# A row norm in a decoder trunk: rstd on all partitions from one product with ones, and a power over 128x256

## The chip, the cores and the metric

The kernel runs on one core of a Trainium2 chip. The metric is the device time of one execution in microseconds (us). A core has TensorE (PE in the profile, its weight loads PEld), VectorE (DVE), ScalarE (ACT), GpSimd (POOL) and SyncE (SP), which issues the transfers. Each engine takes its instructions in order; an instruction that waits holds everything behind it on its engine.

## The reference

A two-layer decoder trunk on one sequence of 256 tokens and 1024 features, in f32. Layer 0 mixes tokens with latent attention (MLA), layer 1 with a Mamba-2 scan (SSD); each mixer stands between two SwiGLU networks of half a step. So there are six sub-layers, numbered s = 0 to 5 here: FFN, MLA, FFN, FFN, SSD, FFN. Each begins with the norm

```
def rms_norm(x, gain):
    y = xf * lax.rsqrt(jnp.mean(xf * xf, axis=-1, keepdims=True) + EPS)
    return y * gain
def modulate(x, gain, mod):
    return rms_norm(x, gain) * (1 + mod[:, None, 1]) + mod[:, None, 0]
...
    x = x + 0.5 * m[:, None, 0, 2] * swiglu(h, ffn_w_gu[i, 0], ffn_w_down[i, 0])
```

and the SSD mixer ends with the same norm over each of 4 groups of 512 gated features, before its output projection. The number that the change is about is rstd = (mean of squares + EPS) to the power -1/2: one number for each token, and for the groups one for each token and group.

## The kernel before

Features lie on the 128 partitions and the 256 tokens run along a tile, so x is 8 tiles of 128x256 and a sum over features is a sum over partitions. Weights come as 1 MB transfers, two pieces of 128x1024 each. A piece is split into a rounded part `whi` (ACT, L205) and the rest `wlo` (DVE, L206), and each product is done in three (`mm3`), so one piece, a 128-wide output tile, is 24 products on PE. `piece()` keeps two pieces split ahead of the one in use.

A sub-layer doesn't wait for its norm. While the sub-layer before leaves x (`leave_chunk`), `enter_chunk` makes raw tiles x times scale, and the squares of x are summed over the 8 tiles into `ssum` (128x256). The first products run on these raw tiles with two extra columns for the shift; their results are multiplied by the rstd row `R` (128x256, the same on every partition) on the way out of PSUM (L421, L523, L526, L764, L1125). Meanwhile `norm_chunks` makes normalised tiles `X2` out of x and R (L421, ACT L422, split L328 and L329), and from the sixth pair of FFN tiles on (NDEF), or the sixth SSD tile (SDEF), the products run on those.

R is made in these steps, at the head of s = 1 to 5:
- `rstd_cols`: two PE products with `ssum` as weights and one column of ones (128x1 each) put the sums of the tokens on partitions; DVE L435 makes mean plus EPS on 128x2; POOL L439 takes the power on 128x2.
- `spread`: two products of that column, broadcast to 128 wide, with the identity bring it back as a row on all partitions (128x256 in PSUM).
- `spread_row`: ACT L453 copies it to SBUF as R.

The four gates of SSD (`gate(g)`, generators that are stepped between the projections and then between the pieces of the output projection `down`) do the same for their groups: squares on ACT (L1419), sums on POOL or DVE (L1423), `rstd_cols`, some steps later `spread`, then L1434 multiplies four tiles by the row in PSUM, and four splits make the input of the output projection. MLA has two further `rstd_cols` (L435, L439 again) for its latents; they stay.

The order of each engine's instructions is made by a scheduler when the program is built: an instruction is taken when its inputs are expected to be ready, except where `order` or `pin` keeps the written order. DVE's queue holds the weight splits L206, the modulation sums L236, the readers of R and the splits of the tiles, all in one line.

Of the kernel before, what the change touches and what calls it, by code (L numbers as in the profile page):

```python
# [12 lines left out]
ALU = mybir.AluOpType  # L13
AX = mybir.AxisListType

D = 1024
T = 256
# [4 lines left out]
EPS = 1e-6  # L22
# [41 lines left out]
class Trunk:  # L64
# [349 lines left out]

    def norm_chunks(self, s, R, ms):

# [25 lines left out]
    def spread(self, r):  # L442
# [4 lines left out]
                             start=True, stop=True)  # L447
        return ps

    def spread_row(self, r):  # L450
        ps = self.spread(r)
        R = self.small([128, T], "R", 1)
        self.nc.scalar.copy(out=R, in_=ps[:, 0:T])  # L453
        return R

# [74 lines left out]
    def ffn(self, s):  # L530
        H = []

        def evac(banks, R):
            H.append(self.split_act(self.ffn_act(banks[0], banks[1], R)))

        if s == 0:
            X, prev = self.open_first(lambda banks: evac(banks, None))
            prevR = None
            j0 = NOPEN
        else:  # L540
            X = self.Xn
            prev = self.proj_first(X, [128, 128])
            r = self.rstd_cols([self.ssum], D)
            X2 = []
            j0 = 1
        for j in range(j0, NJ):
            if s == 0 and j == SETUP_AT:
                self.mla_setup()
            if s and j == NDEF:
                X = X2  # L550
            cur = []
            for i in range(2):
                w = self.piece()
                ps = self.bank()
                self.proj(ps, w, X)
                cur.append(ps)
                if s and j == 1 and i == 0:
                    prevR = R = self.spread_row(r)
                if s and i and 1 <= j < NDEF:
                    X2 += self.norm_chunks(s, R, part(j, NDEF))  # L560
            evac(prev, prevR)
            if s and j == NDEF:
                prevR = None
            if not s or j > NDEF:
                self.ada_half(1 if s else 2)
            prev = cur
        self.down(s, NJ, lambda k: H[k], [lambda: evac(prev, None)], 2, 1, 2)
# [226 lines left out]
    def mla(self, s):  # L794
        nc = self.nc
# [9 lines left out]


        kvp = self.proj_first(X, [128, 128])
        r = self.rstd_cols([self.ssum], D)
        rp = self.bank()
        self.proj(rp, self.piece(), X, 32)  # L810
        R = self.spread_row(r)
        qp = [self.bank()]
        self.proj(qp[0], self.piece(), X)
        kv = [self.latent(kvp[i], R, i) for i in range(2)]
# [531 lines left out]
    def ssd(self, s):  # L1346
        nc = self.nc
        X, X2 = self.Xn, []
        scans, gates = [], []
        done = dict(conv=0, scan=-1, z=0, gate=0)  # L1350

        def step(n=1):

            self.pin = True
            for _ in range(n):
                for line in (scans, gates):
                    if line is gates and done["gate"] >= done["scan"]:
                        continue
                    while line:
                        try:  # L1360
                            next(line[0])
                            break
                        except StopIteration:
                            line.pop(0)
                            done["scan" if line is scans else "gate"] += 1
                            if line is gates:
                                break
            self.pin = False

        pend, raws, xs_all, Z, G = [], [], [], [], []  # L1370
        dst = []
        dtp, ps = self.proj_first(X, [32, 128])
        r = self.rstd_cols([self.ssum], D)
        R = None

        pair = {}

        def evac(kind, i, ps, deferred, direct=False):

            if i % 2 == 0:  # L1380
                pair[kind] = self.slot()
            c0 = (i % 2) * T
            v = pair[kind][:, c0:c0 + T]
            open_pair = [t for t in raws if t[0] is pair[kind]]
            if open_pair:
                open_pair[0][2] = c0 + T
            elif not direct:
                raws.append([pair[kind], c0, c0 + T])
            if kind == "c":
                g, q = divmod(i, 6)  # L1390
                self.conv_evac(ps, R if deferred else None, (16 + g, 20 + g, 4 * g, 4 * g + 1, 4 * g + 2, 4 * g + 3)[q], v)
                dst.append(v)
            else:
                nc.scalar.activation(out=v, in_=ps[:, 0:T], func=AF.Silu if direct else AF.Copy)  # L1394
                Z.append(v)

        def flush():

            for t, c0, c1 in raws:
                self.order(nc.scalar.activation(out=t[:, c0:c1], in_=t[:, c0:c1], func=AF.Silu))  # L1400
            raws.clear()
            done["z"] = len(Z)

        opened = []

        def open_gates():
            while len(opened) < done["conv"] and done["z"] >= 4 * (len(opened) + 1):
                gates.append(gate(len(opened)))
                opened.append(1)

        def gate(g):
            sqs = []
            for ch in range(4 * g, 4 * g + 4):
                y = xs_all[ch]
                nc.vector.tensor_tensor(out=y, in0=y, in1=Z[ch], op=ALU.mult)
            yield
            for i in range(4):
                sq = self.t1()
                nc.scalar.activation(out=sq, in_=xs_all[4 * g + i], func=AF.Square)  # L1419
                sqs.append(sq)  # L1420
            add = nc.vector if g > 1 else nc.gpsimd
            for i in range(3):
                add.tensor_tensor(out=sqs[0], in0=sqs[0], in1=sqs[i + 1], op=ALU.add)  # L1423
            yield
            yield
            r = self.rstd_cols(sqs[:1], 512)
            yield
            yield
            ps = self.spread(r)
            yield  # L1430
            for i in range(4):
                ch = 4 * g + i
                y = xs_all[ch]
                nc.vector.scalar_tensor_tensor(out=y, in0=y, scalar=self.sng[:, ch:ch + 1], in1=ps[:, 0:T],  # L1434
                                               op0=ALU.mult, op1=ALU.mult)
                if i == 1:
                    yield
            for i in range(4):
                G.append(self.split_act(xs_all[4 * g + i]))
                if i == 1:  # L1440
                    yield

        order, c, z = [], 0, 0
        for kind in SSD_ORDER:
            order.append((kind, c if kind == "c" else z))
            c, z = c + (kind == "c"), z + (kind == "z")
        for n, (kind, i) in enumerate(order):
            step(SSD_STEPS[0])
            if n:
                ps = self.bank()  # L1450
                self.proj(ps, self.piece(), X)
            if n == 1:
                R = self.spread_row(r)
            if n == DT_AT:
                scans.append(self.ssd_dt(dtp, R))
            if pend:
                evac(*pend.pop(0))
            pend.append((kind, i, ps, n < SDEF, c == 24 and kind == "z" and i >= ZRAW))
            if 1 <= n < SDEF:
                X2 += self.norm_chunks(s, R, part(n, SDEF))  # L1460
            if n == SDEF - 1:
                X = X2
            step(SSD_STEPS[1])
            if dst and len(dst) % 6 == 0 and len(dst) // 6 > done["conv"]:
                g = done["conv"]
                flush()
                cv = dst[6 * g:]
                xs_all += cv[2:]
                scans.append(self.ssd_group(g, cv[0], cv[1], cv[2:]))
                done["conv"] += 1  # L1470
                open_gates()
            if kind == "z" and i == ZRAW:
                flush()
            if kind == "z" and i >= ZRAW:
                done["z"] = len(Z)
                open_gates()
                self.ada_half()

        def last_evac():
            evac(*pend.pop(0))  # L1480
            done["z"] = len(Z)
            open_gates()

        def finish():
            while scans or gates:
                step()

        def until(n):
            while len(G) < n:
                step()  # L1490
        self.down(s, 16, lambda k: G[k], [last_evac] + [step] * SSD_HOOKS + [finish], 4, SSD_EARLY, 1, SSD_EVERY,
                  [(lambda: until(8), 8), (lambda: until(12), 12)])
# [95 lines left out]
```

## Time and profile before

| | us |
|---|---|
| three runs | 1088.69, 1090.51, 1090.56; median 1090.51 |
| profiled execution | 1090.35 |
| its span in the trace | 1088.6 |
| PE busy | 1067.0 (98%) |
| DVE busy | 871.5 (80%) |
| ACT busy | 627.4 (58%) |
| POOL busy | 40.2 (4%) |

The span is first to last instruction of the profiled execution; 1.75 us of its time lie around it. Busy shares are means over stages. A row of a grouped view gives busy us, the mean ns of one instruction and the idle time of the engine before them with what ended it. A row of a timeline gives start, length, engine, line, operation, tiles and count, and in brackets the idle time before.

### The profile page before, as it was taken

The numbers are of one execution on the slowest core, as the hardware profiler recorded it, in microseconds if no ns is written. First come the engines' busy times: TensorE is split into PE (matmuls) and PEld (weight loads), VectorE is DVE, ScalarE is ACT, GpSimd is POOL, SyncE is SP. The second block draws the span as 40 slices with busy tenths as digits, with TensorE's granted clock in tenths as the row PEclk, the third lists the DMA queues.
The fourth block names the chain that finished last, engine by engine and source line by source line (L and its number), as shares of the span: only waits on it lengthen the run. The fifth ranks groups of instructions, "written<-read, shape, count | busy, mean of one in ns | idle before, by whom it ended". The sixth has DMA issues, their size and how long they took to land.

```text
span 1088.6 us, 21773 instructions
## 1 busy us (share of the span) xinstructions
PE 1067.0 (98%) x8830; PEld 1047.5 (96%) x8830; DVE 871.5 (80%) x1551; ACT 627.4 (58%) x1106; POOL 40.2 (4%) x102
## 2 busy tenths in 40 slices
PE   6999999999999999999999999999999999999998
PEld 5999999998899999999999999999999899999998
DVE  5889998789889888766999886599997788756642
ACT  4564544467667454444754444498898766544431
POOL 0000010000000000000000000000211000000000
PEclk9999999999999999999999999999999999999999
DMA  9988998755266788775699886544344456556630
GB/s 352 345 318 335 349 343 325 257 202 194 81 229 233 285 329 286 284 287 194 232 345 356 332 328 251 172 177 156 117 136 155 141 179 217 200 214 216 233 131 20
DMA packets 38264, 259.59 MB, mean 238 GB/s; under 512 B 4370, under 2 KB 5522, under 8 KB 8084
## 3 DMA queue, kind: packets, MB, share of 16 engines
q1 hardware_dynamic: 38164, 258.21, 65.1%
q8 instruction: 69, 1.13, 0.4%
q14 instruction: 31, 0.25, 0.1%
HBM read 257.14 MB, written 1.05 MB: 237 GB/s over the span
## 4 chain that ended last, share of the span: by engine, by line
PE 90%; ACT 4%; DVE 4%; DMA 1%; issue 0%; SPq 0%; ACTq 0%
PE bank L294 89%; DVE raw L258 2%; PE bank L299 1%; DVE wlo L613 1%; DMA cst<-in_cst_dram 1%; ACT whi L625 1%; ACT whi L205 1%; ACT sl L663 0%; ACT L1394 0%; ACT L1249 0%; ACT dec L1268 0%; ACT t L993 0%; ACT L1268 0%; ACT dec L1249 0%; DVE dec L1272 0%
## 5 line engine op out<-in xcount | busy, mean ns | idle before, releaser
L294 PE MATMUL bank<-sl,whi 128*128 128x256 f32 (+2 forms) x5360 | 957.5, 282 | 2.8 <-ACT whi L205 1.5
L294 PEld LDWEIGHTS bank<-sl,whi 128*128 128x128 f32 (+1 forms) x5360 | 820.0, 188 | 5.9 <-ACT whi L205 1.9
L294 PE MATMUL bank<-sl,wlo 128*128 128x256 f32 (+2 forms) x2680 | 749.9, 282 | 1.6 <-DVE wlo L206 0.9
L205 ACT CAST whi<-raw 128x1024 fp32r<-128x1024 f32 (+1 forms) x329 | 341.2, 1040 | 314.0 <-PE bank L294 224.2
L294 PEld LDWEIGHTS bank<-sl,wlo 128*128 128x128 f32 (+1 forms) x2680 | 504.6, 189 | 3.7 <-DVE wlo L613 2.4
L206 DVE TENSOR_TENSOR wlo<-raw,whi 128x1024 fp32r<-128x1024 f32 (+1 forms) x329 | 397.5, 1212 | 96.7 <-ACT whi L205 95.1
L236 DVE SCALAR_TENSOR_TENSOR raw<-raw,cb 128x1024 f32<-128x1024 f32 x128 | 154.8, 1219 | 23.9 <-DMA raw<-in_adaw_dram 23.8
L328 ACT CAST sl<-t 128x256 fp32r<-128x256 f32 x125 | 48.7, 402 | 27.6 <-DVE t L520 18.8
L329 DVE TENSOR_TENSOR sl<-t,sl 128x256 fp32r<-128x256 f32 x125 | 50.9, 416 | 1.3 <-ACT sl L328 1.3
L459 DVE SCALAR_TENSOR_TENSOR x<-bank,mod,x 128x256 f32<-128x256 f32 x48 | 22.9, 480 | 23.8 <-PE bank L294 23.6
L520 DVE TENSOR_TENSOR t<-t,bank 128x256 f32<-128x256 f32 x70 | 29.0, 416 | 15.0 <-PE bank L294 13.4
L409 ACT ACTIVATE sl<-x,scol 128x256 fp32r<-128x256 f32 x40 | 20.3, 508 | 27.8 <-DVE x L459 27.7
L1130 DVE SCALAR_TENSOR_TENSOR sl<-t,cst,sl 128x256 f32<-128x256 f32 x72 | 34.5, 489 | 0.2
L519 ACT ACTIVATE t<-bank 128x256 f32<-128x256 f32 x70 | 26.4, 377 | 2.9 <-PE bank L294 2.9
L294 PE MATMUL bank<-whi,sl 128*128 128x384 f32 (+1 forms) x80 | 24.3, 369 | 0.0
L408 POOL CAST sl<-bspl 128x4 fp32r<-128x4 f32 x40 | 11.6, 337 | 317.7 <-PE bank L294 117.3
L613 DVE TENSOR_TENSOR wlo<-raw,whi 128x1024 fp32r<-128x1024 f32 (+1 forms) x17 | 19.7, 1162 | 3.8 <-ACT whi L625 3.7
L439 POOL TENSOR_TENSOR rr<-rv,mhalf 128x2 f32<-128x2 f32 x11 | 11.0, 1001 | 312.7 <-DVE rv L435 312.7
L410 DVE SCALAR_TENSOR_TENSOR sl<-x,scol,sl 128x256 fp32r<-128x256 f32 x40 | 19.1, 481 | 4.1 <-ACT sl L409 4.0
L1268 ACT ACTIVATE dec<-sl,nac 128x128 f32<-128x128 f32 x64 | 20.5, 394 | 2.6 <-DVE sl L1257 2.5
L299 PE MATMUL bank<-ident,t 128*96 128x128 f32 (+2 forms) x116 | 18.2, 274 | 3.4 <-ACT t L993 3.4
L422 ACT ACTIVATE t<-t,mod,scol 128x256 f32<-128x256 f32 x32 | 18.2, 595 | 5.3 <-DVE t L421 5.3
(217 smaller groups left out, 665.6 us busy)
## 6 DMA issues: line engine op xcount, KB each, us to landing
raw<-in_wgu_dram SPq DMA_DIRECT2D x80, 1024.0 KB, 5.4
raw<-in_adaw_dram SPq DMA_DIRECT2D x64, 1024.0 KB, 5.7
raw<-in_wdn_dram SPq DMA_DIRECT2D x44, 1024.0 KB, 6.6
raw<-in_win_dram SPq DMA_DIRECT2D x19, 1024.0 KB, 4.9
raw<-in_wout_dram SPq DMA_DIRECT2D x8, 1024.0 KB, 4.8
raw<-in_adao_dram SPq DMA_DIRECT2D x6, 1024.0 KB, 6.8
raw<-in_wop_dram SPq DMA_DIRECT2D x6, 1024.0 KB, 7.4
raw<-in_mwo_dram SPq DMA_DIRECT2D x4, 1024.0 KB, 5.0
```

Source lines behind the costliest of these rows:

```text
L205: self.nc.scalar.copy(out=hi, in_=raw)
L206: self.nc.vector.tensor_tensor(out=lo, in0=raw, in1=hi.bitcast(F32), op=ALU.subtract)
L236: nc.vector.scalar_tensor_tensor(out=w, in0=w, scalar=1.0, in1=self.cb, op0=ALU.mult, op1=ALU.mult, accum_out=self.mod[:, q, 2 * u + i:2 * ...
L294: ins = self.nc.tensor.matmul(*a, **k)
L299: ins = self.nc.tensor.transpose(*a, **k)
L328: self.nc.scalar.copy(out=hi, in_=src)
L329: self.nc.vector.tensor_tensor(out=lo, in0=src, in1=hi.bitcast(F32), op=ALU.subtract)
L459: nc.vector.scalar_tensor_tensor(out=self.x[m], in0=ps[:, 0:T], scalar=self.mod[:, q, m:m + 1], in1=self.x[m], op0=ALU.mult, op1=ALU.add)
L519: nc.scalar.activation(out=tg, in_=pg[:, 0:T], func=AF.Silu)
L520: nc.vector.tensor_tensor(out=tg, in0=tg, in1=pu[:, 0:T], op=ALU.mult)
L613: order(nc.vector.tensor_tensor(out=w[2][i][:, o], in0=raw, in1=w[1][i][:, o].bitcast(F32), op=ALU.subtract))
L1130: nc.vector.scalar_tensor_tensor(out=dst, in0=u[:, t:t + T], scalar=cw[:, t:t + 1], in1=dst, op0=ALU.mult, op1=ALU.add)
```

## The change

`rstd_rows` takes the place of `rstd_cols` and `spread` at the five heads and in the four gates. One product with a 128x128 matrix of ones as weights and the 128x256 squares as moving data puts the sum of each token on every partition. Mean plus EPS is then taken by DVE on 128x256, out of PSUM, and the power by POOL on 128x256, in place. The result is R itself (or, in a gate, a tile that L1434, now L1441, reads from SBUF).

```diff
+    def rstd_rows(self, sq, n, row):
+        nc = self.nc
+        ps = self.bank()
+        self.matmul(ps[:, 0:T], self.ones, sq, start=True, stop=True)
+        nc.vector.tensor_scalar(out=row, in0=ps[:, 0:T], scalar1=1.0 / n, scalar2=EPS, op0=ALU.mult, op1=ALU.add)
+        nc.gpsimd.tensor_tensor(out=row, in0=row, in1=self.mhalf[:, 0:1].broadcast_to([128, T]), op=ALU.pow)
+        return row
+
+    def rstd_row(self, sq, n):
+        return self.rstd_rows(sq, n, self.small([128, T], "R", 1))
...
-            r = self.rstd_cols([self.ssum], D)
+            prevR = R = self.rstd_row(self.ssum, D)
...
-                if s and j == 1 and i == 0:
-                    prevR = R = self.spread_row(r)
...
-            r = self.rstd_cols(sqs[:1], 512)
+            row = self.rstd_rows(sqs[0], 512, self.t1())
             yield
             yield
-            ps = self.spread(r)
             yield
...
-                nc.vector.scalar_tensor_tensor(out=y, in0=y, scalar=self.sng[:, ch:ch + 1], in1=ps[:, 0:T],
+                nc.vector.scalar_tensor_tensor(out=y, in0=y, scalar=self.sng[:, ch:ch + 1], in1=row,
```

MLA and SSD heads are edited as the FFN head is. In the changed kernel the mean is L455 and the power L456; the readers of R L523, L526 are L535, L538, and L1434 is L1441.

DVE at the head of s = 2 before: `rv` is the mean, `R` the spread row, `wlo` a weight split.

```order
L435 TENSOR_SCALAR rv_4127<-bank_4124 128x2 [waits PE_49]
L206 TENSOR_TENSOR wlo_4166<-raw_3785,whi_4165 128x1024 [waits Activation_49]
L206 TENSOR_TENSOR wlo_4214<-raw_3870,whi_4213 128x1024 [waits DMAHW6_49,Activation_49]
L236 SCALAR_TENSOR_TENSOR raw_4169,mod<-raw_4169,cb 128x1024 [waits DMAHW2_49]
L206 TENSOR_TENSOR wlo_4243<-raw_3870,whi_4242 128x1024 [waits PE_49,Activation_49]
L421 TENSOR_TENSOR t_714_4196<-x_69,R_4163 128x256 [waits Activation_49]
```

The same place in the changed kernel:

```order
L455 TENSOR_SCALAR R_4117<-bank_4118 128x256 [waits PE_49]
L206 TENSOR_TENSOR wlo_4152<-raw_3778,whi_4151 128x1024 [waits Activation_49]
L421 TENSOR_TENSOR t_708_4182<-x_69,R_4117 128x256 [waits Pool_49]
L535 TENSOR_TENSOR t_710_4188<-bank_4067,R_4117 128x256 [waits Activation_49]
L538 TENSOR_TENSOR t_712_4193<-bank_4068,R_4117 128x256
L206 TENSOR_TENSOR wlo_4200<-raw_3863,whi_4199 128x1024 [waits DMAHW6_49,Activation_49]
```

Between the mean and the first reader of R there stood three splits and a modulation sum; now one split stands there, and the others stand behind the reader, which waits for POOL.

DVE at the last gate (g = 3) before, where `bank_11084` is the spread row in PSUM:

```order
L435 TENSOR_SCALAR rv_11046<-bank_11043 128x2 [waits PE_49]
L1434 SCALAR_TENSOR_TENSOR sl_10192<-sl_10192,cst,bank_11084 128x256 [waits PE_49]
L1434 SCALAR_TENSOR_TENSOR sl_10192<-sl_10192,cst,bank_11084 128x256
L1434 SCALAR_TENSOR_TENSOR sl_10355<-sl_10355,cst,bank_11084 128x256 x2
L329 TENSOR_TENSOR sl_11091<-sl_10192,sl_11091 128x256 [waits Activation_49]
```

And now:

```order
L455 TENSOR_SCALAR t_1704_11000<-bank_11001 128x256 [waits PE_49]
L1441 SCALAR_TENSOR_TENSOR sl_10159<-sl_10159,cst,t_1704_11000 128x256 [waits Pool_49]
L1441 SCALAR_TENSOR_TENSOR sl_10159<-sl_10159,cst,t_1704_11000 128x256
L1441 SCALAR_TENSOR_TENSOR sl_10322<-sl_10322,cst,t_1704_11000 128x256 x2
L329 TENSOR_TENSOR sl_11043<-sl_10159,sl_11043 128x256 [waits Activation_49]
```

Nothing moved here; the wait for PE has become a wait for POOL, with nothing in between in either.

## Rows read from the trace of the kernel before

**Rows 1.** The page: busy time of PE, and the chain by engine.
```profile
PE 1067.0 (98%) x8830; PEld 1047.5 (96%) x8830; DVE 871.5 (80%) x1551; ACT 627.4 (58%) x1106; POOL 40.2 (4%) x102
...
PE 90%; ACT 4%; DVE 4%; DMA 1%; issue 0%; SPq 0%; ACTq 0%
```

**Rows 2.** Windows at two FFN heads: length, busy PE, PEld, DVE, ACT, POOL, clock.
```profile
326.00:355.00 29.00, 29.00 (x242) 29.00 (x241) 28.21 (x53) 22.49 (x45) 0.69 (x1) 1.00 0.63 220
...
903.00:932.00 29.00, 29.00 (x244) 29.00 (x243) 27.50 (x52) 22.45 (x44) 1.69 (x1) 1.00 0.63 218
```

**Rows 3.** Timeline of PE at the head of s = 2.
```profile
325.56 0.50 PE L294 MATMUL bank<-ones,ssum 128*128 128x1 f32 x4
325.92 0.48 PE L294 MATMUL bank<-sl,whi 128*128 128x258 f32 x2
326.24 0.28 PE L294 MATMUL bank<-sl,wlo 128*128 128x258 f32 x1
...
328.90 0.61 PE L294 MATMUL bank<-ident,rr 128*128 128x128 f32 x4
```

**Rows 4.** Groups by line and shape: ACT copy, DVE mean, a wide DVE operation.
```profile
L767 DVE TENSOR_SCALAR t<-t,bcol,cst 128x256 f32<-128x256 f32 x5 | 2.0, 410 | 0.0
...
L453 ACT COPY R<-bank 128x256 f32<-128x256 f32 x5 | 1.8, 365 | 0.0
...
L435 DVE TENSOR_SCALAR rv<-bank 128x2 f32<-128x2 f32 x11 | 1.7, 155 | 14.4 <-PE bank L294 14.4
```

**Rows 5.** Groups by line and shape on POOL.
```profile
L439 POOL TENSOR_TENSOR rr<-rv,mhalf 128x2 f32<-128x2 f32 x11 | 11.0, 1001 | 312.7 <-DVE rv L435 312.7
L1423 POOL TENSOR_TENSOR t<-t,t 128x256 f32<-128x256 f32 x6 | 6.0, 1002 | 37.5 <-ACT t L1419 37.5
...
L1120 POOL MEMSET t<- 128x3 f32 x24 | 2.0, 100 | 86.0 <-ACT t L993 50.3 <-ACT bcol L334 15.7 <-DVE sl L1130 5.2
```

**Rows 6.** Timeline of POOL: an addition and two powers.
```profile
822.25 0.74 POOL L1423 TENSOR_TENSOR t<-t,t 128x256 f32<-128x256 f32 x1 [15.39 <-ACT t L1419]
825.53 1.63 POOL L439 TENSOR_TENSOR rr<-rv,mhalf 128x2 f32<-128x2 f32 x1 [2.54 <-DVE rv L435]
...
869.06 0.69 POOL L439 TENSOR_TENSOR rr<-rv,mhalf 128x2 f32<-128x2 f32 x1 [21.89 <-DVE rv L435]
```

**Rows 7.** Timeline of DVE: means and first readers of the spread row.
```profile
217.15 0.16 DVE L435 TENSOR_SCALAR rv<-bank 128x2 f32<-128x2 f32 x1 [0.80 <-PE bank L294]
...
224.63 0.75 DVE L764 TENSOR_TENSOR t<-bank,R 128x256 f32<-128x256 f32 x2
...
326.10 0.16 DVE L435 TENSOR_SCALAR rv<-bank 128x2 f32<-128x2 f32 x1 [2.54 <-PE bank L294]
326.41 2.36 DVE L206 TENSOR_TENSOR wlo<-raw,whi 128x1024 fp32r<-128x1024 f32 x2 [0.16 <-ACT whi L205]
...
330.12 1.22 DVE L206 TENSOR_TENSOR wlo<-raw,whi 128x1024 fp32r<-128x1024 f32 x1 [0.20 <-ACT whi L205]
331.26 0.42 DVE L421 TENSOR_TENSOR t<-x,R 128x256 f32<-128x256 f32 x1
...
778.82 0.14 DVE L435 TENSOR_SCALAR rv<-bank 128x2 f32<-128x2 f32 x1
...
782.67 0.46 DVE L1434 SCALAR_TENSOR_TENSOR sl<-sl,cst,bank 128x256 f32<-128x256 f32 x1
...
868.82 0.16 DVE L435 TENSOR_SCALAR rv<-bank 128x2 f32<-128x2 f32 x1 [0.92 <-PE bank L294]
870.56 1.66 DVE L1434 SCALAR_TENSOR_TENSOR sl<-sl,cst,bank 128x256 f32<-128x256 f32 x4 [1.57 <-PE bank L294]
...
902.69 0.16 DVE L435 TENSOR_SCALAR rv<-bank 128x2 f32<-128x2 f32 x1 [3.23 <-PE bank L294]
...
907.76 0.42 DVE L421 TENSOR_TENSOR t<-x,R 128x256 f32<-128x256 f32 x1
```

**Rows 8.** Timeline of PE at the last gate: the sum, and the wait.
```profile
868.28 0.50 PE L294 MATMUL bank<-ones,t 128*128 128x1 f32 x4
...
871.53 0.85 PE L294 MATMUL bank<-sl,whi 128*128 128x256 f32 x5 [1.01 <-ACT sl L328]
```

More of the change, by code (lines that the diff above doesn't have):

```diff
@@ L807, in mla @@
         kvp = self.proj_first(X, [128, 128])
-        r = self.rstd_cols([self.ssum], D)
+        R = self.rstd_row(self.ssum, D)
         rp = self.bank()
         self.proj(rp, self.piece(), X, 32)
-        R = self.spread_row(r)
         qp = [self.bank()]
@@ L1372, in ssd @@
         dtp, ps = self.proj_first(X, [32, 128])
-        r = self.rstd_cols([self.ssum], D)
-        R = None
+        R = self.rstd_row(self.ssum, D)
         pair = {}
@@ L1451, in ssd @@
                 self.proj(ps, self.piece(), X)
-            if n == 1:
-                R = self.spread_row(r)
             if n == DT_AT:
```

## The prediction

> **What bounds the kernel now.** I read the page first. PE is busy for 98% of the span and 90% of the chain that ended last is PE [rows 1], so whatever leaves PE's line is a gain and whatever makes PE wait is a loss, nearly at its full length. Next I read the stretches where the norms are made. At the FFN heads PE and its loads have no idle time at all, and DVE is busy for 28.21 of 29.00 us at s = 2 and 27.50 at s = 5 [rows 2]: a delay of DVE there finds almost no idle time to be made up in. Then the timelines of PE, POOL and DVE, for what a norm costs and for how long its result lies ready before somebody reads it.
>
> **The change part by part.** It makes nine norms in another way: five heads and four gates.
>
> *PE.* At the head of s = 2 the pair of products after the column sums starts at 325.56, and the second record behind it at 326.24, where it would follow after some 0.24 without them; the column sums thus cost 0.44 us of PE, and the spread has the same four records and much the same length (0.61 against 0.50) [rows 3]. The new product also streams 256 columns of f32 in two records, as the spread's two did, so I price it as the spread: 0.44. It costs at least nothing and at most the two together, 0.88. So PE saves 0.44 us per norm, 9 x 0.44 = 4.0 us (bounds 0 and 7.9).
>
> *ACT.* Five copies of 0.365 go, 1.8 us [rows 4]. ACT has idle time at the heads (22.5 of 29 us busy [rows 2]), so I count nothing.
>
> *DVE.* The mean on 128x256 costs about what L767 costs, 0.41, in place of 0.155 [rows 4]: 9 x 0.255 = 2.3 us more on DVE. It is part of the chain below and not counted a second time.
>
> *POOL.* The power goes from 2 columns to 256. This is the one large unknown. The trace has a power on 2 columns alone: 0.69 us undisturbed, 1.63 where POOL had to share its time with other work nearby [rows 6], 1.00 in the mean of eleven [rows 5]. It has an addition on 256 columns: 0.74 [rows 6]. And a memset of 3 columns: 0.10, which I take for the bare cost of an instruction [rows 5]. From below, the wide power can't beat the wide addition by much: 0.74. From above, all of the 0.59 us that the small power takes beyond the bare instruction goes by the column: 0.295 each, 256 x 0.295 + 0.10 = 75.6 us. The ends are a factor of 100 apart. The row that is nearest is the power itself, since it is the same operation; an addition of 256 columns costs (0.74 - 0.10) / 256 = 2.5 ns a column, and two columns at that price are 5 ns, so 0.58 us of the small power is work that an addition doesn't have. I take a third of the 0.59 for entering and leaving the routine and two thirds for the columns, an estimate: 0.195 a column, 0.10 + 0.20 + 256 x 0.195 = 50 us. Call the length P.
>
> *The path.* What has to be known is how late R may come. Before, the mean was ready for DVE at 326.10 and the first reader of R ran at 331.26, 5.16 us later, since splits were put in between. At the other heads the gap is 7.48 (217.15 to 224.63, MLA), 5.66, 5.16 and 5.07 (902.69 to 907.76), together 28.5; at the four gates 3.85 (778.82 to 782.67), 4.28, 5.24 and 1.74 (868.82 to 870.56), together 15.1 [rows 7] (of the nine pairs, the first and the last of each kind and s = 2 stand there). After the change the gap is 0.41 for the wide mean, some 0.1 for each of two hand-offs (the power at 869.06 starts 0.08 after the mean at 868.82 + 0.16 [rows 6, 7]), and P. So norm i delays its first reader by P - (gap - 0.6). The nine slacks are 6.9, 4.6, 5.1, 4.6, 4.5 and 3.3, 3.7, 4.6, 1.1: 38.2 us together.
>
> A delayed reader delays PE because of what is queued behind it. In the order of the changed kernel the reader that waits for POOL stands one split behind the mean; two splits and a modulation sum that were done in the gap before now stand behind the wait, and so do all later splits. PE has the pieces that were split ahead, then the first one whose `wlo` is not there stops it. ACT is held too, since its next operations read what the waiting DVE instructions write. As DVE is at 97% of the stretch [rows 2], the delay isn't worked off before PE needs the normalised tiles. At the last gate there is no cover at all: PE already waits 1.01 us for the casts behind L1434 [rows 8].
>
> *The sum.* Against the profiled execution's own 1090.35 us (the median of the runs shown is 1090.51, 0.16 more): 1090.35 - 4.0 + 9P - 38.2 = 1048.15 + 9P, where P is above all slacks. With P = 50.2: 1048.15 + 451.8 = 1500 us.
>
> The Trainium skill speaks against this edit in general: "GPSIMD Engine Reference", in its introduction, calls the engine the wrong choice for ordinary elementwise arithmetic, and the section "Performance pitfalls for Q7 kernels" gives a chain of dependent f32 operations 4 cycles a step. No run here shows the chain inside the power; the 0.59 us for two columns agrees with a long one.
>
> **The rivals.**
>
> *The power is cheap (faster).* If the 0.59 us is all entry and the columns stream as the addition's do, P is 0.74, below every slack, and nobody waits: 1090.35 - 4.0 = 1086.3. For it: the addition's 2.5 ns a column; eleven small powers can't tell an entry from a column. Against it: an addition, a memset and a power of few columns differ by their arithmetic, and the small power takes almost seven times the bare instruction. The point from which it is decided: stalls eat the 4.0 us at P = 4.05 (2.9 at the last gate, 0.8 and 0.4 at the first two), that is at 15 ns a column. [...]
>
> *The columns are pipelined, but at a price.* The routine works on several columns at once, and P lies between 5 and 30 us. The geometric mean of the two, 12.2, gives 1048.15 + 110 = 1158. For it: nothing in the rows excludes it, and two columns are too few to fill a pipeline. Against it: the two columns would then have to cost nearly the same as one.
>
> *DVE and POOL get in each other's way.* Additions and powers on POOL show 1.0 us in the mean where 0.69 to 0.74 is the undisturbed length, and one power took 1.63 [rows 5, 6], so up to 0.94 us per norm may come on top, 8.5 us. It is no case of its own, since DVE mostly stands still while the wide power runs; it widens each case upward.
>
> **How the numbers follow.** A column price near that of the small power (P of 30 to 75): 0.48, and the likeliest; its own range is 1418 to 1723. Pipelined (P of 4 to 30): 0.34. Cheap (P under 4): 0.18. The range takes in the cheap end at 1086, which is a bound of the unknown price and almost 2 in 10 by itself; at the top I leave out the last few us of P (71 and more): 1690. What this measurement can tell from no change is about 0.2%, 2.2 us. The time is 2.2 below at stalls under 1.8 us, P under 2.9: 0.15. It is within at P of 2.9 to 4.65: 0.03. The rest is slower: 0.82.
>
> **What would show it.** The row of L456 on POOL gives P at once. Right: DVE idles at each of nine places with the wait ended by POOL R (or t) L456, PE's idle time is about 38 us short of nine times P, and POOL's busy time rises from 40 us by 9P. The slacks are wrong if PE's idle time at the heads begins sooner or later than some 5 us into the power. The forecast is wrong if L456 takes a few us: then PE's busy time is down by about 4 us and little else is to be seen. That the scheduler put the waiting reader only one split behind the mean is what turns P into a stall; if PE's waits end at something else than DVE's splits, that step failed.

## The result, and the profile after

| | before | after |
|---|---|---|
| median of 6 runs each, us | 1089.84 (1088.69 to 1090.74) | 1443.63 (1439.77 to 1446.87) |
| profiled execution, us | 1090.35 | 1439.77 |
| span, us | 1088.6 | 1438.0 |
| mean granted clock of TensorE | 0.998 | 0.880 |

The ratio is 1.3246 (95% interval 1.3227 to 1.3264): slower by a third. The forecast was 1500 in a range of 1086 to 1690.

The page of the changed kernel: busy time by engine and the chain by engine, which answer to [rows 1].

```profile
PE 1090.8 (76%) x8776; PEld 1065.8 (74%) x8776; DVE 871.7 (61%) x1551; ACT 621.8 (43%) x1101; POOL 409.8 (29%) x102
...
PE 54%; POOL 23%; DVE 10%; ACT 4%; issue 3%; POOLq 3%; DMA 2%; SPq 0%; DVEq 0%; ACTq 0%
```

POOL has come into the chain with 23%. PE's busy time has not fallen by a few us but risen by 23.8, and its idle time (span less busy) went from 21.6 to 347.2 us. The two together, 325.6 + 23.8 = 349.4, are the whole difference of the spans.

The groups of POOL, after (busy us, mean ns, idle time before), answer to [rows 5]:

```profile
L456 POOL TENSOR_TENSOR R<-R,mhalf 128x256 f32<-128x256 f32 x5 | 210.0, 41992 | 255.9 <-DVE R L455 255.9
L456 POOL TENSOR_TENSOR t<-t,mhalf 128x256 f32<-128x256 f32 x4 | 166.0, 41512 | 42.3 <-DVE t L455 42.3
```

That is P: 42.0 us at a head, 41.5 at a gate, 376.0 in all. The wide mean is as cheap as it was priced [rows 4]:

```profile
L455 DVE TENSOR_SCALAR R<-bank 128x256 f32<-128x256 f32 x5 | 2.1, 424 | 10.2 <-PE bank L294 10.2
```

Now the head of s = 2 on DVE, in the timeline (start, length, ..., idle time before), as in [rows 7]:

```profile
365.48 0.42 DVE L455 TENSOR_SCALAR R<-bank 128x256 f32<-128x256 f32 x1 [2.64 <-PE bank L294]
365.82 1.22 DVE L206 TENSOR_TENSOR wlo<-raw,whi 128x1024 fp32r<-128x1024 f32 x1
408.06 0.42 DVE L421 TENSOR_TENSOR t<-x,R 128x256 f32<-128x256 f32 x1 [41.02 <-POOL R L456]
...
409.06 1.21 DVE L206 TENSOR_TENSOR wlo<-raw,whi 128x1024 fp32r<-128x1024 f32 x1
```

and the power on POOL, which took 0.7 to 1.6 us on two columns [rows 6]:

```profile
366.05 41.97 POOL L456 TENSOR_TENSOR R<-R,mhalf 128x256 f32<-128x256 f32 x1 [26.75 <-DVE R L455]
...
1141.53 41.12 POOL L456 TENSOR_TENSOR t<-t,mhalf 128x256 f32<-128x256 f32 x1 [23.18 <-DVE t L455]
```

The second row is the power of the last gate, beside which DVE stands idle: 41.12.

PE at the same head, the sum product and the end of its wait, beside [rows 3]:

```profile
364.72 0.28 PE L294 MATMUL bank<-sl,wlo 128*128 128x258 f32 x1
364.84 0.60 PE L294 MATMUL bank<-ssum,ones 128*128 128x256 f32 x2
365.09 0.60 PE L294 MATMUL bank<-sl,whi 128*128 128x258 f32 x2
365.53 0.28 PE L294 MATMUL bank<-sl,wlo 128*128 128x258 f32 x1
...
410.33 0.58 PE L294 MATMUL bank<-sl,wlo 128*128 128x258 f32 x1 [33.05 <-DVE wlo L206]
```

This is the stall as the prediction drew it. The reader L421 waits for POOL; the next weight split, L206, stands behind it and runs at 409.06; PE's first product with the `wlo` of that split can't start before 410.33. PE had run on for 11.2 us after the power began (410.33 - 33.05 - 366.05), then stood still. At the last gate there is nearly no cover; the row answers to [rows 8], where the wait was 1.01 us:

```profile
1183.68 1.67 PE L294 MATMUL bank<-sl,whi 128*128 128x256 f32 x6 [41.58 <-ACT sl L328]
```

The waits of DVE for POOL, in sum, times and the longest: nine, as many as there are norms.

```profile
DVE sl L1441 <- POOL t L456: 162.4, 4, 41.3
DVE t L421 <- POOL R L456: 123.0, 3, 41.0
...
DVE t L774 <- POOL R L456: 41.0, 1, 41.0
DVE t L1134 <- POOL R L456: 41.0, 1, 41.0
```

And what PE waited for:

```profile
PE bank L294 <- DVE wlo L206: 140.7, 4, 40.0
PE bank L294 <- ACT sl L328: 78.4, 4, 41.6
PE bank L294 <- DVE dec L1281: 38.2, 4, 36.6
PE bank L294 <- DVE sl L1266: 32.8, 1, 32.8
PE bank L294 <- ACT t L776: 32.1, 1, 32.1
```

Last, the clock. These are windows of the same head, to be set against [rows 2]: length; busy time and count for PE, PEld, DVE, ACT, POOL; granted clock of TensorE; share of the DMA engines; GB/s.

```profile
370.00:375.00 5.00, 5.00 (x44) 5.00 (x43) 0.00 (x0) 0.00 (x0) 5.00 (x1) 1.00 0.26 105
...
380.00:409.00 29.00, 0.00 (x0) 0.00 (x0) 0.94 (x3) 0.48 (x1) 28.02 (x1) 0.50 0.00 0
409.00:413.00 4.00, 2.67 (x12) 2.67 (x13) 3.98 (x9) 3.97 (x8) 0.00 (x0) 0.50 0.00 0
413.00:417.00 4.00, 4.00 (x34) 4.00 (x33) 4.00 (x8) 3.49 (x8) 0.00 (x0) 0.95 0.40 106
```

While PE idles, the granted clock is 0.50, the 1.2 GHz level, and at this head it stays there for about the first 3 us after the wait: 12 products in 2.67 us, 0.22 each, where at the 2.4 GHz level there are 44 in 5.00 us, 0.11 each. I summed PE's busy time times (1 - granted clock) over windows of 5 us: 1.5 us before, 28.1 after. That is 26.6 us more, where the busy time rose by 23.8; I put the 2.8 between them down to the shorter norm. By the records of the granted clock, PE works for 3.1 (this head) to 8.8 us (s = 4) at the low level after each of the nine waits, and half of that is lost: 1.5 to 4.4 us a wait, 23 in all. The other 5 us go in three drops of the clock at 304, 529 and 1076 us, each behind a wait of PE of only 1.7 to 2.3 us.

### The profile page after: what moved, and what is told of

Same layout as the page of the kernel before. It is cut to its first block, busy times and chain, and to the rows that moved or that the text cites. A ratio compares the mean times of both kernels' runs of the same rounds, so it can differ in the third digit from the quotient of the medians.

```text
span 1438.0 us, 21643 instructions
## 1 busy us (share of the span) xinstructions
PE 1090.8 (76%) x8776; PEld 1065.8 (74%) x8776; DVE 871.7 (61%) x1551; ACT 621.8 (43%) x1101; POOL 409.8 (29%) x102
## 4 chain that ended last, share of the span: by engine, by line
PE 54%; POOL 23%; DVE 10%; ACT 4%; issue 3%; POOLq 3%; DMA 2%; SPq 0%; DVEq 0%; ACTq 0%
PE bank L294 54%; POOL R L456 12%; POOL t L456 12%; POOLq L1588 3%; DVE wlo L206 2%; DMA raw<-in_adaw_dram 1%; DVE raw L258 1%; DVE sl L1139 1%; DVE wlo L623 1%; DVE raw L236 1%; PE bank L299 1%; ACT dec L1277 1%; ACT whi L205 1%; DMA cst<-in_cst_dram 0%; ACT whi L635 0%
## 5 line engine op out<-in xcount | busy, mean ns | idle before, releaser
L294 PE MATMUL bank<-sl,whi 128*128 128x256 f32 (+2 forms) x5360 | 976.1, 285 | 115.1 <-ACT sl L328 78.4
L294 PEld LDWEIGHTS bank<-sl,whi 128*128 128x128 f32 (+1 forms) x5360 | 835.0, 191 | 121.0 <-ACT sl L328 79.4
L294 PE MATMUL bank<-sl,wlo 128*128 128x256 f32 (+2 forms) x2680 | 757.2, 284 | 141.2 <-DVE wlo L206 140.7
L294 PEld LDWEIGHTS bank<-sl,wlo 128*128 128x128 f32 (+1 forms) x2680 | 512.1, 192 | 143.5 <-DVE wlo L206 141.5
L206 DVE TENSOR_TENSOR wlo<-raw,whi 128x1024 fp32r<-128x1024 f32 (+1 forms) x329 | 397.5, 1212 | 78.2 <-ACT whi L205 77.2
L456 POOL TENSOR_TENSOR R<-R,mhalf 128x256 f32<-128x256 f32 x5 | 210.0, 41992 | 255.9 <-DVE R L455 255.9
L456 POOL TENSOR_TENSOR t<-t,mhalf 128x256 f32<-128x256 f32 x4 | 166.0, 41512 | 42.3 <-DVE t L455 42.3
L1441 DVE SCALAR_TENSOR_TENSOR sl<-sl,cst,t 128x256 f32<-128x256 f32 x16 | 6.8, 483 | 162.4 <-POOL t L456 162.4
L421 DVE TENSOR_TENSOR t<-x,R 128x256 f32<-128x256 f32 x32 | 12.5, 418 | 123.0 <-POOL R L456 123.0
L294 PE MATMUL bank<-dec,sl 128*64 128x256 f32 (+1 forms) x128 | 14.6, 350 | 38.2 <-DVE dec L1281 38.2
L1277 ACT ACTIVATE dec<-sl,nac 128x128 f32<-128x128 f32 x64 | 20.5, 395 | 46.1 <-DVE sl L1266 45.9
L294 PEld LDWEIGHTS bank<-dec,sl 128*64 128x64 f32 x128 | 8.3, 141 | 43.3 <-DVE dec L1281 36.8
L471 DVE SCALAR_TENSOR_TENSOR x<-bank,mod,x 128x256 f32<-128x256 f32 x48 | 22.9, 480 | 26.3 <-PE bank L294 26.2
```

Of the source, the lines that this page charges most:

```text
L206: self.nc.vector.tensor_tensor(out=lo, in0=raw, in1=hi.bitcast(F32), op=ALU.subtract)
L294: ins = self.nc.tensor.matmul(*a, **k)
L456: nc.gpsimd.tensor_tensor(out=row, in0=row, in1=self.mhalf[:, 0:1].broadcast_to([128, T]), op=ALU.pow)
L471: nc.vector.scalar_tensor_tensor(out=self.x[m], in0=ps[:, 0:T], scalar=self.mod[:, q, m:m + 1], in1=self.x[m], op0=ALU.mult, op1=ALU.add)
L1277: self.order(nc.scalar.activation(out=t[:, j, 2 * c], in_=q[:, o:o + 128], func=AF.Exp, bias=self.nac[:, c, h:h + 1]))
```

## The experiments

**Rstd without a power.** POOL multiplies the 128x256 row by zeros in the place of the power, so the output is useless; the instructions stand in the same order.

```diff
-        nc.gpsimd.tensor_tensor(out=row, in0=row, in1=self.mhalf[:, 0:1].broadcast_to([128, T]), op=ALU.pow)
+        nc.gpsimd.tensor_tensor(out=row, in0=row, in1=self.zero[:, 0:1].broadcast_to([128, T]), op=ALU.mult)
```

> The changed kernel with one operation replaced: POOL multiplies the 128x256 row by zeros instead of taking the power, so rstd is 0 everywhere; the order of instructions on PE, DVE and ACT is that of the changed kernel. Theory (all of the loss is the length of the power, 42 us nine times; the rest of the change saves 0.44 us of PE nine times): the row of POOL falls to about 0.74 us, PE's waits at the nine places vanish, and the time is 1086 us (1084 to 1088), 0.3 to 0.5% under the kernel before. Rival (the earlier place of the waiting reader and the wide mean on DVE cost something by themselves): 1090 or more, with waits of PE for DVE at the heads.

Measured: 1094.41 us (12 runs, 1089.37 to 1097.52), ratio 1.0028 (1.0012 to 1.0044). So 349 of the 354 us are the power. But the rest, the form of the change without its price, is a loss of 4 us and not a gain of 4. The theory missed. The rival's time came out, but not its place: past the first 20 us PE's waits of over 1 us, the longest 1.72, are in the latent attention and at the gates, not at the heads. On POOL, by groups and then two single rows:

```profile
L458 POOL TENSOR_TENSOR R<-R,zero 128x256 f32<-128x256 f32 x5 | 7.4, 1483 | 249.5 <-DVE R L457 249.5
L458 POOL TENSOR_TENSOR t<-t,zero 128x256 f32<-128x256 f32 x4 | 4.0, 1002 | 41.7 <-DVE t L457 41.7
...
874.96 0.61 POOL L458 TENSOR_TENSOR t<-t,zero 128x256 f32<-128x256 f32 x1 [22.45 <-DVE t L457]
908.13 1.52 POOL L458 TENSOR_TENSOR R<-R,zero 128x256 f32<-128x256 f32 x1 [29.21 <-DVE R L457]
```

The multiplication takes 0.61 us at the two gates where DVE stands idle beside it, and 1.26 to 1.53 at the seven places where DVE works beside it.

Nothing waits long, yet PE idles 24.5 us (21.6 before), and its busy time is 1068.3 against 1067.0. Part of that is the clock; a short gap of PE at 295.93 (1.51 us, behind an exponential of the latent attention) and the windows around it:

```profile
288.00:296.00 8.00, 6.49 (x57) 5.91 (x56) 6.63 (x23) 4.32 (x16) 0.40 (x4) 1.00 0.00 0
296.00:300.00 4.00, 4.00 (x22) 4.00 (x23) 2.50 (x6) 1.69 (x7) 0.36 (x4) 0.55 0.74 262
300.00:304.00 4.00, 4.00 (x24) 4.00 (x23) 2.62 (x5) 0.58 (x1) 0.37 (x5) 0.60 0.14 16
304.00:308.00 4.00, 4.00 (x36) 4.00 (x36) 2.26 (x3) 0.59 (x1) 1.85 (x7) 1.00 0.63 250
```

22 and 24 products in 4 us, then 36 again. Over the run 4.7 us more than before are lost to the low level. The twelve runs go with it: five at a mean clock of 0.997 or 0.998 took 1089.4 to 1091.5 us, seven at 0.991 to 0.994 took 1094.4 to 1097.5. The three at 0.998 (1089.4 to 1089.7) lie some 0.9 us under the eleven runs of the kernel before at 0.998 (1090.2 to 1090.6). The kernel before has the same kind of gap in its latent attention (1.42 us) and no such drop in its profile, and after the change a gap of the same 1.51 us at 332.28 brought none; why one gap brings the drop and another doesn't stays open.

**The price by column.** The power on the first k columns; the other columns get a constant by one more DVE instruction (k = 24, 64, 128). With it the scheduler orders DVE and ACT a little otherwise than in the change, in all three alike.

```diff
-        nc.vector.tensor_scalar(out=row, in0=ps[:, 0:T], scalar1=1.0 / n, scalar2=EPS, op0=ALU.mult, op1=ALU.add)
-        nc.gpsimd.tensor_tensor(out=row, in0=row, in1=self.mhalf[:, 0:1].broadcast_to([128, T]), op=ALU.pow)
+        nc.vector.tensor_scalar(out=row[:, 0:24], in0=ps[:, 0:24], scalar1=1.0 / n, scalar2=EPS, op0=ALU.mult, op1=ALU.add)
+        nc.vector.tensor_scalar(out=row[:, 24:T], in0=ps[:, 24:T], scalar1=0.0, scalar2=0.02, op0=ALU.mult, op1=ALU.add)
+        nc.gpsimd.tensor_tensor(out=row[:, 0:24], in0=row[:, 0:24], in1=self.mhalf[:, 0:1].broadcast_to([128, 24]), op=ALU.pow)
```

> The power on 24 of the 256 columns (the other columns of the row get a constant, by one more VectorE instruction of about 0.4 us at each place), everything else as in the change. Theory 'price by column' (0.365 us + 0.163 us per column): the power takes 4.3 us, less than what TensorE has left to do at seven of the nine places, so nearly all of the 350 us go: 1091 to 1097 us, 9 x 4.3 = 39 us of power for at most 7 us of time. Rival 'the first column costs most' (a price for the instruction, whatever its width): the power still takes over 30 us and the kernel over 1300 us.

> The power on 64 of the 256 columns, the rest a constant, everything else as in the change. Theory 'price by column': 10.8 us a power. By the leads that the trace of the change shows (54 us over the nine places, at most 9.3 at one) TensorE idles about 42 us more than before: 1128 to 1133 us, and up to 1158 if every wait brings the lower clock. By the leads of the prediction (38 us in all) it idles 59 us more: 1145 us without the clock. Rival 'price of the instruction': over 1300 us.

> The power on 128 of the 256 columns, the rest a constant. Theory 'price by column': 21.2 us a power, TensorE idles 137 us more than before by the leads seen in the trace of the change (153 by those of the prediction): 1225 us without a cost of the clock, 1250 with the 28 us that the change showed. Rival 'price of the instruction': over 1300 us.

Measured: 1110.13 us (4 runs, ratio 1.0177, 1.0150 to 1.0204), 1155.53 (4 runs, 1.0593, 1.0567 to 1.0620) and 1254.60 (2 runs, 1.1508, 1.1473 to 1.1542). The powers of the three kernels, in their groups at the heads:

```profile
L457 POOL TENSOR_TENSOR R<-R,mhalf 128x24 f32<-128x24 f32 x5 | 20.8, 4158 | 253.0 <-DVE R L455 253.0
```

```profile
L457 POOL TENSOR_TENSOR R<-R,mhalf 128x64 f32<-128x64 f32 x5 | 52.6, 10523 | 253.8 <-DVE R L455 253.8
```

```profile
L457 POOL TENSOR_TENSOR R<-R,mhalf 128x128 f32<-128x128 f32 x5 | 106.7, 21348 | 254.7 <-DVE R L455 254.7
```

With 24 and 64 columns all nine powers have one length; with 128 and 256 they differ by up to 1.0 us, and the last gate, where DVE is idle beside the power, has the shortest, 20.72 and 41.12. The shortest lie on a straight line: (41.12 - 4.16) / 232 = 0.159 us a column and 0.33 for the rest, which gives 10.5 at 64 and 20.7 at 128, and 0.65 at the 2 columns of before, where 0.69 was read. The rival, a price of the instruction whatever its width, is out. How a power turns into time is seen when the runs stand side by side (us; PE's idle and busy time against before; the clock's part by the sum over windows):

| one power, head / gate | nine of them | PE idles more | hidden | PE busy more | the clock's part |
|---|---|---|---|---|---|
| 1.48 / 1.00 (zeros) | 11.4 | 2.9 | 8.5 | 1.3 | 4.7 |
| 4.16 / 4.16 (24 columns) | 37.4 | 11.2 | 26.2 | 8.7 | 12.3 |
| 10.52 / 10.53 (64) | 94.7 | 46.5 | 48.2 | 19.9 | 20.5 |
| 21.35 / 20.72 (128) | 189.6 | 138.6 | 51.0 | 26.9 | 30.0 |
| 41.99 / 41.51 (256) | 376.0 | 325.6 | 50.4 | 23.8 | 26.6 |

What PE can hide stops at some 50 us for nine places; beyond it every us of power is a us of time. The clock's part hardly grows with the wait, 20 to 30 us from 64 columns on, so short waits are dear: with 24 columns I expected 1091 to 1097 and missed by 13, since I had counted 7 us of gaps and no clock. Of what the low level costs there, 8.5 us fall in the latent attention, around 280 and 300 us, behind gaps of 1.07 and 1.51 us. With 64 columns the idle time (46.5) lies near the leads read from the trace of the change (42), not near those of the prediction (59); the time is near the expected top of 1158. With 128 columns idle time (138.6 for 137) and time (1254.6 for 1250) came out nearly as expected.

**Heads alone, gates alone.** The gates, or the heads, as in the kernel before.

```diff
-            row = self.rstd_rows(sqs[0], 512, self.t1())
+            r = self.rstd_cols(sqs[:1], 512)
...
+            row = self.spread(r)[:, 0:T]
```

> The change at the five heads only, the gates as before. Theory (each place pays for itself: PE's waits at the heads of the changed kernel are 33.1, 33.1, 34.5, 36.7 and 33.1 us, 170.4 together, plus some 2 us each at the low clock, less 5 x 0.44): 1090 + 170 + 10 - 2 = 1268 us (1260 to 1275). Rival (places share cost, as a stall lets DVE and the transfers run ahead and so shortens the next): the two halves don't add up, outside 1250 to 1285.

> The change at the four gates of the state-space layer alone, the five heads as before. Theory 'the places add up': the change has lost 353 us against before and the heads alone 195, so this loses about 158: 1248 us (1243 to 1253). Of it TensorE idles 36.6 + 0.9 + 32.8 + 40.0 + 41.6 = 152 us at the gates, less about 2 that it idled there before, and some 10 us are matmuls at the lower clock behind four waits. Rival 'the gates' waits hide one another or the heads': clearly less than 150 us lost.

Measured: heads 1285.59 us (2 runs, ratio 1.1791, 1.1771 to 1.1811), gates 1247.99 (2 runs, 1.1448, 1.1427 to 1.1469). Heads alone lose 195.2 us, gates alone 157.7, together 352.9; the change lost 353.8. The places add up. The heads' time alone would not have settled it: it lies outside the theory's 1260 to 1275 and just past the 1285 from which I had given it to the rival. I was 18 us low there: PE idles 175 us more, where I had 170, and its busy time is up by 19, where I had 8. PE's busy time with the heads changed, and then with the gates changed:

```profile
PE 1086.3 (85%) x8800; PEld 1061.7 (83%) x8800; DVE 870.8 (68%) x1551; ACT 621.5 (48%) x1101; POOL 246.1 (19%) x102
```

```profile
PE 1073.5 (86%) x8806; PEld 1053.4 (85%) x8806; DVE 873.4 (70%) x1551; ACT 627.7 (50%) x1106; POOL 204.1 (16%) x102
```

**One more piece split ahead.**

```diff
-AHEAD = 2
+AHEAD = 3
```

> The changed kernel with three weight pieces split ahead instead of two. At the heads of s = 1, 2, 3 and 5 one more split stands ahead of the reader that waits for POOL. Theory (PE stops at the first piece whose low part is queued behind the waiting reader): PE gets one piece, 2.87 us, further at those four heads, its waits there fall from about 33 to about 30 us, and the time falls by some 11 us to 1429 (1425 to 1434). Rival (PE stops for want of a PSUM bank or of the normalised tiles): the waits stay at 33 to 34.5 us and the time at 1440.

Measured: 1430.40 us (2 runs, 1426.69 and 1434.12), ratio 1.3119 (1.3086 to 1.3153), a time as expected, though the two runs lie 7 us apart. At s = 2 the wait of PE is 2.4 us shorter than after the change (33.05 there); the second row is the wait at s = 1:

```profile
407.48 0.58 PE L294 MATMUL bank<-sl,wlo 128*128 128x258 f32 x1 [30.62 <-DVE wlo L206]
...
259.25 1.87 PE L294 MATMUL bank<-ones,t 128*128 128x1 f32 x8 [32.11 <-ACT t L776]
```

At s = 3 and 5 the wait is shorter by 3.0 and 2.5 us as well, so at these three heads PE's lead is the stock of split pieces, and the stall ends with the first split behind the waiting reader. At s = 1 I had expected the same, but the wait stayed at 32.11 us, as after the change; it doesn't end at a split, and nor does the one at s = 4, which moved by 0.3. So 7.8 of the 13 us come from the three heads; the rest is spread over the gates and smaller gaps.

**PE kept busy through the wait.** Useless products behind each sum product.

```diff
+        junk = self.bank()
+        for _ in range(fill):
+            self.matmul(junk[:, 0:T], self.ones, sq, start=True, stop=True)
```

> The change as it stands, with useless products of the matrix of ones and the squares put right behind each of the nine sum products (72 at a head of a layer, 82, 72, 88 and 90 at the four gates, by about 0.44 us each, into a bank that nothing reads), so that TensorE works for most of the time in which it stood idle. Theory 'clock': of the 23.8 us by which TensorE's busy time grew, about 28 come from matmuls at the 1.2 GHz level behind the nine waits, and they go: 1412 to 1420 us, the granted clock back at about 0.99. Rival 'the waits are all': the added products only fill time in which nothing could be done, and the end stays at 1440 us (1436 to 1448); were the fillers longer than the waits, it would be more.

Measured: 1485.55 us (4 runs, 1480.26 to 1491.92), ratio 1.3620 (1.3562 to 1.3679): both theories missed. The fill did its work: PE's idle time fell from 347.2 to 95.6. But without the 692 added products (0.434 each, 300 us) PE's busy time is 1391.2 - 300.3 = 1090.9, as after the change, so the clock gave next to nothing back; the fillers' 300 us stand where 252 us of idle time went, and the rest is added time. At s = 2 the clock held through the wait, and then fell after gaps of 1.97 and 1.64 us in which PE waited for the next splits (18 products in 3.47 us, 0.19 each):

```profile
411.00:423.00 12.00, 12.00 (x99) 11.92 (x98) 0.00 (x0) 0.00 (x0) 12.00 (x1) 1.00 0.00 0
423.00:428.00 5.00, 3.03 (x25) 2.83 (x24) 4.75 (x9) 4.29 (x9) 0.19 (x1) 1.00 0.00 0
428.00:434.00 6.00, 3.47 (x18) 3.06 (x17) 5.64 (x13) 3.54 (x9) 0.00 (x0) 0.80 0.43 158
```

And the fillers moved other work. In the latent attention DVE now takes modulation sums, which wait for their transfers, ahead of an operation that PE waits for (L831; as L828 of the change it ran at 261.72, before them). PE's wait of 18.69 us there is new. On DVE:

```profile
270.25 1.22 DVE L236 SCALAR_TENSOR_TENSOR raw<-raw,cb 128x1024 f32<-128x1024 f32 x1 [2.49 <-DMA raw<-in_adaw_dram]
...
277.53 1.22 DVE L236 SCALAR_TENSOR_TENSOR raw<-raw,cb 128x1024 f32<-128x1024 f32 x1 [4.91 <-DMA raw<-in_adaw_dram]
...
280.27 0.35 DVE L831 TENSOR_SCALAR t<-t,bank 32x256 f32<-32x256 f32 x1
```

So this run doesn't say what the change would take with the clock held up; that stays open.

**The same product, with rstd on ACT.** At the heads alone, the gates as before, then at all nine.

```diff
-        nc.vector.tensor_scalar(out=row, in0=ps[:, 0:T], scalar1=1.0 / n, scalar2=EPS, op0=ALU.mult, op1=ALU.add)
-        nc.gpsimd.tensor_tensor(out=row, in0=row, in1=self.mhalf[:, 0:1].broadcast_to([128, T]), op=ALU.pow)
+        self.order(nc.scalar.activation(out=row, in_=ps[:, 0:T], func=AF.Ln, scale=1.0 / n, bias=self.epsc))
+        self.order(nc.scalar.activation(out=row, in_=row, func=AF.Exp, scale=-0.5))
```

> The product with ones at the five heads, but rstd taken on ACT as the exponential of -1/2 times the logarithm, both on 128x256 (some 0.5 us each), with the logarithm's table loaded ahead of the last casts; the four gates as in the kernel before. Theory (only the length of the step counts, and ACT's some 3.5 us with its table loads stay under the slacks of 5 to 9 us): 5 x 0.44 us less on PE, 1087.5 us (1085.5 to 1089.5). Rival (the tables hold up the weight casts that stand behind them on ACT): PE waits for casts at the heads, 1091 to 1100.

> The product with ones at all nine places, and rstd taken by ScalarE alone (logarithm, then the exponential of minus one half of it, on 128x256, straight from PSUM) with no VectorE and no GpSimd instruction between; the heads alone so took 1088.2 us against 1090.4. Theory 'the power is the whole loss, and the idea would pay': at each gate the product of columns and the products that spread go, TensorE's busy time falls by about 1 us more than with the heads alone, and the two ScalarE instructions with a table load (about 2.1 us where the power took 41.5) end inside the leads of gates 0, 1 and 2 and about 1 us behind that of gate 3: 1086 to 1089 us. Rival 'the gates live on small margins': ScalarE is the busiest there, the table loads (1.28 us each) delay the operands of the scan, and one or two short gaps bring a low clock of 2 to 3 us each: 1091 to 1096 us.

Measured: heads alone 1088.22 us (11 runs, 1087.96 to 1089.76), ratio 0.9981 (0.9972 to 0.9990), the fastest kernel here, inside the theory's range; all nine 1090.32 (11 runs, 1088.52 to 1093.03), ratio 1.0001 (0.9990 to 1.0012). In the kernel with the heads alone the two steps take 0.9 us where the power took 42, and PE's busy time is 1064.5, 2.5 under before:

```profile
L460 ACT ACTIVATE R<-bank,epsc 128x256 f32<-128x256 f32 x5 | 2.3, 469 | 0.0
...
L461 ACT ACTIVATE R<-R 128x256 f32<-128x256 f32 x5 | 2.1, 425 | 0.0
```

Of these 2.5 us, though, 1.7 aren't the change's. In the profile of the kernel before the clock drops for 3.4 us at 67 us, long ahead of the first head that is changed (217 us); here it doesn't, with the same products in PE's order up to there. The windows around it, before and with the heads on ACT:

```profile
65.00:70.00 5.00, 4.10 (x22) 3.87 (x22) 5.00 (x8) 3.59 (x6) 0.00 (x0) 0.71 0.51 175
...
65.00:70.00 5.00, 4.13 (x32) 3.92 (x33) 5.00 (x8) 4.29 (x9) 0.00 (x0) 1.00 0.52 205
```

The runs show the same. At a mean clock of 0.999 or 1.000 nine runs with the heads on ACT took 1088.0 to 1088.4 us and eight of the kernel before 1088.8 to 1089.2; at 0.998 two took 1089.6 and 1089.8, and eleven before 1090.2 to 1090.6. So at the same clock the heads gain 0.7 to 0.8 us, a third of the 2.2 that were expected; the rest of the 2.1 us between the medians is that more of the runs before had a lower clock, which isn't shown to come from the norms. Why the gain isn't 2.2 stays open.

With all nine PE's busy time falls further, to 1062.8, but its idle time is 24.7 against 21.7; two of the gaps at the gates:

```profile
849.00 0.39 PE L294 MATMUL bank<-sl,wlo 128*128 128x256 f32 x1 [1.25 <-DVE wlo L206]
...
854.24 0.50 PE L294 MATMUL bank<-sl,whi 128*128 128x256 f32 x2 [0.86 <-ACT whi L205]
```

That goes in the rival's direction (small margins at the gates), though its time, 1091 to 1096, wasn't reached, nor was the theory's 1086 to 1089. What gain there is, is at the heads.

## Why the prediction was right, and where it was off

*The number.* The range of 1086 to 1690 took in all but the top of what was thought possible, so that the time lies in it says little. The point, 1500, was 60 us above the profiled execution, and that is the sum of errors that partly cancel, below.

*Mechanism.* It held in the main: nine waits of DVE for POOL; PE stopped by what stands behind the waiting reader; nothing worked off later. PE's idle time rose by 325.6 where nine powers are 376.0, and L456 gave P at once. One step of it failed by the prediction's own sign at five places: that PE's waits would end at DVE's splits held at four of nine (s = 2, 3, 5 and the third gate, 140.7 us). At the others PE waited for casts (s = 4 and the last gate), the scan's operands (the first two gates) and the square in the latent attention, all of them in DVE's queue behind a waiting reader or made from what stands there. The five waits are of the same size, 32.1 to 41.6 us against 33.1 to 40.0, so the time came out much the same.

*P.* Forecast 50.2, measured 41.8 in the mean: 75.8 us too much over nine. The choice was the right one of three: the power costs by the column, at nearly the price of the small power. I had split the small power's 0.59 us into one third of entry and two thirds for two columns, 0.195 each; it is 0.159 each. That the split came so near was luck: no row of the kernel before could tell a third from none or all, and none and all were 0.74 and 75.6, the bounds, which held.

*The leads.* Forecast 38.2 in all, measured 50.4 net of the idle time before: 12.2 too little. I had read them off DVE (mean to first reader), and said that idle time would begin about 5 us into the power. At s = 2 it began at 11.2 us, and its end came 2.3 us after the power's, so the lead is 8.9 and not 4.6. At s = 2, 3 and 5 PE's own stock of split pieces is the lead; the run with a third piece moved it.

*The clock.* The sum had no term for it: 26.6 us. This is the step that the prediction lacks. Its error was hidden by that of P: with P as measured, and the rest as forecast, the sum gives 1424 for the profiled execution's 1440.

*PE's saving.* Forecast 4.0. The sum product at s = 2 delays the products behind it by 0.45 us (365.53, where 365.08 would follow), as priced; over nine norms some 2.8 us come out, but only by difference, as what is left when the clock is taken off.

Together: 75.8 less for P, 12.2 less for the leads, 26.6 more for the clock, 1.2 more for the saving, all against +409.6, make +349.4, the measured difference of the spans. It must close, as the saving was taken by difference.

*The rivals.* Cheap power: P is 42. Pipelined columns: P is above its 5 to 30. But the cheap case was mis-sized as well: with a short POOL step the kernel took 1094.4 and not 1086.3, since the gaps and the clock ate the saving. Contention of DVE and POOL: lengths of the kind that it would give are there, and of the size that was given. The power takes 41.12 at the two gates where DVE idles and 41.8 to 42.0 at the seven places where DVE works beside its start, as the multiplication by zeros takes 0.61 and up to 1.53. Over nine powers it is 376.0 - 9 x 41.12 = 5.9 us, where up to 8.5 were allowed. The powers on 24 and 64 columns show nothing of it, so what makes the difference stays open. One slip in the numbers: a P of 30 gives 1048 + 270 = 1318, so the likeliest case begins at 1318 and not at 1418; the range didn't hang on it.

"GPSIMD Engine Reference" of the Trainium skill, section "Performance versus the Vector engine", measures an addition of 2048 elements on GpSimd at 4497 ns, 2.2 ns an element. The runs agree for a multiplication (0.61 us undisturbed, 2.4 ns a column); a power costs 67 times that (41.12), so the figure isn't to be used for it. "TensorE: Matmul & The Clock Gate" of the Trainium skill, section "HAM oscillation — how this bites in real kernels", says that the price of the slow clock is paid anew at every long wait; the nine waits here agree, with 1.5 to 4.4 us lost behind each.

## What to carry to other kernels

Moving an operation from a narrow tile to a wide one is priced by its own rate per column, and a power on GpSimd has one of another order than an addition; where the rate is unknown, the same operation at two widths settles it. A lead is measured on the engine that would stop, as the work it holds ready, not on the queue that is delayed. A long wait on a TensorE that is always busy cost here its length plus 1.5 to 4.4 us of slow clock, and gaps of 1 to 2 us were followed by the low level in some places, so a few of them can eat a saving of 4 us. And a gain of 2 us between medians is to be set against runs of the same clock before it is put down to the change.

## What the runs showed of the hardware

- GpSimd's power on 128 partitions takes 0.159 us a column and about 0.33 besides, from 24 columns (4.16 us) to 256 (41.12, with DVE idle). ScalarE takes the logarithm and the exponential of the same tile in 0.47 and 0.43 us.
- On 128x256 GpSimd took up to 0.9 us longer where VectorE worked beside it: 1.26 to 1.53 us against 0.61 for a multiplication, 41.8 to 42.0 against 41.12 for a power. On 24 and 64 columns the power was the same length at all nine places.
- After the waits of 32 us and more TensorE worked for 3.1 to 8.8 us at the 1.2 GHz level; gaps of 1.5 to 2 us were followed by it in two runs (0.55 and 0.60 of the clock around 300 us with the zeros, 0.80 at 428 to 434 us with the fillers), while a gap of 1.51 us at 332 us after the change was not.
